# A decoder layer on one core: unread banks at set boundaries, a planner that counts two more kinds of work, a bias load on another queue, and half a scaling on another engine

## The chip, the cores and the metric

The kernel runs on 1 core of one Trainium2 chip. The metric is the device time of one execution in microseconds (us). Engines are named as in the profile: PE (TensorE matmul), PEld (its weight loads), DVE (VectorE), ACT (ScalarE), POOL (GpSimd) and SP (SyncE, which here only issues transfers). L12 is line 12 of the kernel before.

## The reference

One layer of a decoder on a sequence of 256 tokens and 2048 channels, in float32: a SwiGLU FFN of width 5632, a mixer with two branches, and a second FFN. A conditioning vector gives nine rows of modulation (`mod`).

```python
mod = (silu(c) @ w_ada + b_ada).reshape(B, 9, 1, D)
h = modulate(rms_norm(x, g_ffn1), mod[:, 0], mod[:, 1])
x = x + 0.5 * mod[:, 2] * swiglu(h, w_ffn1_gu, w_ffn1_down)

h = modulate(rms_norm(x, g_mix), mod[:, 3], mod[:, 4])
u_pool, q, k, v, ga, gb = split(h @ w_in)
y_pool = multiscale_pool(u_pool, pool_mix, pool_scale) @ w_pool_up
y_attn = swa_sink_attention(q, k, v, q_gain, k_gain, sinks, rel_bias) @ w_attn_up
x = x + mod[:, 5] * ((sigmoid(ga) * y_pool + sigmoid(gb) * y_attn) @ w_o)

h = modulate(rms_norm(x, g_ffn2), mod[:, 6], mod[:, 7])
x = x + 0.5 * mod[:, 8] * swiglu(h, w_ffn2_gu, w_ffn2_down)
```

The attention is causal in a window of 128 tokens, in blocks of 128, with 16 heads of 64 channels over 2 key heads, a relative-position bias and one sink logit per head in the softmax.

## The kernel before, in words

**Matmuls in three terms.** Every large product goes through `Set.mm` (L296). A weight tile that has been loaded (`raw`) is cut into a rounded high half `wh` (ACT, L277) and the rest `wl` (DVE, L281); the activations lie as high and low halves too (`hh`, `hl`, or `sh`, `sl` made in L385 and L386). PE computes hi x wh, lo x wh and hi x wl. A *set* is one product of 256 tokens with up to 1024 columns: four banks of the accumulator memory (PSUM) of 512 columns, two for each half of the tokens. The inner dimension goes in *ktiles* of 128 rows; a ktile of a full set is 12 matmuls with 512 columns, one of a 512-column set is 6. There are eight banks in two groups of four. A set has one group, the next set the other; small products in between (sums for the modulation, transposes, attention) take their banks from the group that the current set does not use (`bank`), which is the group that the next set will take.

**The written order.** The scheduler is off: each engine runs its instructions in the order in which the code issues them. `push` queues a ktile's matmuls and runs the *turn* of the ktile two before it (`LAG = 2`): its matmuls, and then whatever was filed under that turn's number with `at(n, f)`. So between the L281 of ktile n + 2 and that of ktile n + 3 DVE runs the extra work of turn n. There are three buffers of `wh` and of `wl`, six of `raw` (`RAW`), three of the scratch tag `t2`.

**Set boundaries.** `ends` holds the turn of each set's last ktile. `hop(n, f, g)` files a product f at turn n and the reading of its bank g at n + 1, and moves both on while n is in `ends`. `with_bank` does the same with a fresh bank.

**The modulation.** mod is a product with one row; DVE does it: for each of 16 slabs of `w_ada` one L223, which adds raw times a scalar to an accumulator `acc` of up to 1024 columns (these are called rows of `w_ada` below; the first of an accumulator may be L221). Then the 128 partitions are summed: `halves` (ACT L186, DVE L187), two matmuls with ones (`prod`, L192 and L193), and `use`: for mod 2, 5 and 8 (the gates) ACT copies the bank into `gate` (L199); for the others `mod_col` turns it into a column of channels with four or five DVE operations (L165, L168, L172 or L174 and L175). For gates POOL clears the accumulator and adds the bias row (L214, L215).

**The planner.** `ada_plan(js, n0)` spreads the rows over turns: `room[n]` (2.6 for a full ktile) less `busy[n]` is what DVE has free, in us, by prices written in the code: 1.22 for a wl, 1.28 for a row, and so on, entered with `will`. `spread` gives out turns as the free time adds up. The price of halves and of the columns is not entered. The first FFN plans mod 2, 4, 3 and the first 1024 columns of 7; the mixer plans mod 5, 6 and the rest of 7; the second FFN plans mod 8. The first FFN ends its gate and up products in narrow sets of 512 columns.

**The mixer** runs these sets: q, k and v (256 columns), u, and then twice: a gate of 1024 columns (GA), pool_up (8 ktiles), a gate (GB), attn_up (8 ktiles); then w_o. `heads(n, g)` files a pair of heads, eight times: the load of the bias (L1095, issued by SP, from a table in DRAM) at turn n - 1, the logits at n and their bias adds (L1057, L1058) at n + 1, the maxima at n + 2, the exponentials (ACT L1072) at n + 3, `over` at n + 4 (reciprocal and four scalings, L1076 to L1080, DVE), the transposes at n + 5 (L1085; copied by ACT, L1092, a turn later), and for each second pair the product with v at n + 7 with its copies (L1122, DVE) at n + 8. There is one bias tile, so the load of a pair waits until DVE has read the bias of the pair before.

**Transitions** from the first FFN to the mixer and from the mixer to the second FFN are written out by hand (`transition`).

Of the kernel before, what the change touches and what calls it, by code (L numbers as in the profile page):

```python
# [16 lines left out]
P = 128  # L17
# [17 lines left out]
T2 = 3  # L35
TAIL = 4
TA, TB = 5, 4
NS = 7
LAG = 2
ROOM = 2.6  # L40


@with_exitstack
def trunk_layer(ctx, tc, x, c, w_ada, b_ada, g_ffn1, w_ffn1_gu, w_ffn1_down, g_mix, w_in,
# [78 lines left out]

    def hop(n, f, g):

        while n in ends:
            n += 1
        at(n, f)
        at(n + 1, g)
# [46 lines left out]

    def ada_plan(js, n0):

        def sums(j, c0, a, n, o):
            got = []

            def halves():
                hi, lo = t_([P, CW], "t2", T2, F32R), t_([P, CW], "t2", T2, F32R)
                nc.scalar.copy(hi, a[0][:, o:o + CW])  # L186
                nc.vector.tensor_tensor(lo, a[0][:, o:o + CW], hi.bitcast(F32), ALU.subtract)  # L187
                got.extend((hi, lo))

            def prod():  # L190
                got.append(bank())
                nc.tensor.matmul(got[2], ones, got[0], start=True, stop=False)  # L192
                nc.tensor.matmul(got[2], ones, got[1], start=False, stop=True)  # L193

            def use():
                if j % 3 == 2:
                    if j not in gates:
                        gates[j] = t_([P, D], "gate", 1)
                    nc.scalar.activation(gates[j][:, c0 + o:c0 + o + CW], got[2], AF.Copy, scale=1.0 if j == 5 else 0.5)  # L199
                else:  # L200
                    mod_col(j, got[2], c0 + o)

            at(n, halves)
            hop(n + 2, prod, use)

        for j, c0, a_w in js:
            a, r, nk = [], [], 2 * SW // a_w
            where = spread(n0, KD, 1.28 * a_w / SW)
            for kk, n in enumerate(where):
# [15 lines left out]
                at(n, go)  # L225
                will(n, 1.28 * a_w / SW)
            n0 = n
# [314 lines left out]
    def ffn(w_gu, w_down, hh, hl, actT, f0, sg, g, jgate, after, js):  # L542
# [13 lines left out]
        for f in range(f0, DFF, SW):  # L556
            u = min(SW, DFF - f) / SW
            for i in range(KD * (1 if first else 2) - (TB if g is not None and f == f0 else 0)):
                room[n], busy[n] = ROOM * u, busy.get(n, 0.0) + 1.22 * u
                n += 1  # L560
# [5 lines left out]
        for i in range(2 * KF):  # L566
            will(n + i, 1.22 + (0.34 if i < KF or not 4 <= i - KF < 4 + KD else 0.0))
# [286 lines left out]
    def toe_out():  # L854
# [55 lines left out]
    for n in range(nQ, W1 + KD - TA):  # L910
        u = 0.26 if nK <= n < nU else 1.0
        room[n] = ROOM * u
        will(n, 1.22 * u)
        if any(a <= n < a + 8 for a in Y + A) or n >= W0:
            will(n, 0.34)
# [32 lines left out]

    def with_bank(n, shape, f, g):

        b = []
        hop(n, lambda: (b.append(bank(shape)), f(b[0])), lambda: g(b[0]))

# [42 lines left out]
    with_bank(nU + 11, (P, CW), k_turn,  # L996
              lambda b: nc.scalar.activation(kT.rearrange("p a b -> p (a b)"), b, AF.Copy, scale=gq[:, 1:2]))
    with_bank(nU + 12, (P, S), v_turn, lambda b: nc.scalar.copy(vR.rearrange("p a b -> p (a b)"), b))

# [43 lines left out]
    def heads(n, g):  # L1043
# [31 lines left out]
        def over():  # L1075
            nc.vector.tensor_tensor(dn, sm, es, ALU.add)  # L1076
            nc.vector.reciprocal(rc, dn)
            for i in range(2):
                for blk, (a, e) in enumerate(spans):
                    nc.vector.tensor_scalar_mul(l[:, i, a:e], l[:, i, a:e], rc[:, blk, i:i + 1])  # L1080

# [6 lines left out]
        def turned(i):  # L1088
            def f(b):
                if g % 2 == i == 0:  # L1090
# [3 lines left out]

        at(n - 1, lambda: nc.sync.dma_start(bias, bass.AP(tensor=toe[:].tensor, offset=toe[:].offset + h0 * TOE,  # L1095
                                                          ap=[[1, P], [TOE, 2], [1, S]])))
# [23 lines left out]
        for blk in range(2):  # L1120
            with_bank(n + 7, (P, 2, P), out_prod(blk),
                      lambda b, blk=blk: nc.vector.tensor_copy(attnT[:, g - 1:g + 1, blk * P:(blk + 1) * P], b))  # L1122
        will(n + 8, 0.8)

# [165 lines left out]
```

## Time and profile before

| what | value |
|---|---|
| median of 3 runs | 2011.06 us (2009.54 to 2015.25) |
| the profiled execution's own time | 2012.3 us |
| its span, first to last instruction | 2010.5 us |
| mean granted clock of PE | 0.998 |
| busy: PE, DVE, ACT, POOL | 1977.7, 1515.2, 1084.2, 20.1 us |
| read from memory (HBM) | 520.00 MB, 260 GB/s over the span |
| first FFN, about | 27 to 775 us |
| mixer, about | 775 to 1277 us |
| second FFN, about | 1277 us to the end |

The profile gives the busy time of each engine, the idle time ahead of each group of instructions with what ended it (`<-`), and who waited for whom. A busy PE is not PE at its peak: the end of a matmul is modelled, and matmuls overlap. Idle time of an engine that the others do not wait for costs nothing. The time of a single execution contains 1.8 us around the span.

### The profile page before, as it was taken

What the parts mean: (1) busy time and instruction counts of PE and PEld (TensorE: products, weight loads), DVE (VectorE), ACT (ScalarE), POOL (GpSimd) and SP (SyncE); (2) the same over time, 40 slices, a digit from 0 to 9 for tenths busy, and PEclk for the clock granted to TensorE, in tenths of its full rate; (3) what the DMA queues carried; (4) which work ended last, traced back from release to release, by engine and by line L of the source; (5) the groups of instructions that cost most, each with busy time, mean ns of one, the idle gap of its engine ahead of it and who ended that gap; (6) DMA issues with size and microseconds to landing.
All of it is one profiled execution on the core that took longest, in us unless ns stands there. A gap on an engine that the chain in (4) does not pass through costs nothing.

```text
span 2010.5 us, 23739 instructions
## 1 busy us (share of the span) xinstructions
PE 1977.7 (98%) x8873; PEld 1629.0 (81%) x8873; DVE 1515.2 (75%) x1759; ACT 1084.2 (54%) x1469; POOL 20.1 (1%) x42
## 2 busy tenths in 40 slices
PE   7999999999999999999999999999999999999998
PEld 5788888888788878887778888888788888888887
DVE  6888877989999988876799996888455454565655
ACT  5544457664655446445556455645554645565443
POOL 1000000000000000000000000000000000000000
PEclk9999999999999999999999999999999999999999
DMA  9989745899899976764698984688555545476652
GB/s 355 381 304 336 261 165 188 329 348 367 320 364 346 326 257 236 292 228 153 232 339 304 370 321 158 225 335 327 212 198 189 210 176 198 152 228 214 218 185 74
DMA packets 159603, 523.67 MB, mean 260 GB/s; under 512 B 9309, under 2 KB 23285, under 8 KB 159232
## 3 DMA queue, kind: packets, MB, share of 16 engines
q1 hardware_dynamic: 158496, 520.92, 72.3%
q8 instruction: 69, 1.13, 0.2%
q0 software_dynamic: 992, 1.24, 0.2%
q14 instruction: 46, 0.38, 0.1%
HBM read 520.00 MB, written 2.12 MB: 260 GB/s over the span
## 4 chain that ended last, share of the span: by engine, by line
PE 89%; DVE 5%; DMA 3%; ACT 1%; issue 1%; SPq 0%; ACTq 0%; DVEq 0%
PE bank L296 86%; DVE wl L281 2%; DMA raw<-in_w_in_dram 1%; DVE acc L223 1%; DMA raw<-in_w_pool_up_dram 1%; ACT wh L277 1%; DMA raw<-in_w_ada_dram 1%; DVE acc L649 0%; PE bank L1024 0%; SPq L641 0%; PE bank L792 0%; DMA raw<-in_w_ffn_down_dram 0%; PE bank L349 0%; PE bank L192 0%; DVE mcol L168 0%
## 5 line engine op out<-in xcount | busy, mean ns | idle before, releaser
L277 ACT CAST wh<-raw 128x1024 fp32r<-128x1024 f32 (+2 forms) x712 | 710.6, 1001 | 805.0 <-PE bank L296 709.8
L281 DVE TENSOR_TENSOR wl<-raw,wh 128x1024 fp32r<-128x1024 f32 (+2 forms) x713 | 822.3, 1156 | 416.5 <-ACT wh L277 409.9
L296 PE MATMUL bank<-wh,hl 128*128 128x512 f32 (+1 forms) x2088 | 654.8, 389 | 0.0
L296 PE MATMUL bank<-wh,hh 128*128 128x512 f32 (+1 forms) x2064 | 651.6, 391 | 2.5 <-ACT gate L199 1.4
L296 PE MATMUL bank<-wl,hh 128*128 128x512 f32 (+1 forms) x2064 | 647.8, 389 | 2.4 <-DVE wl L281 2.3
L296 PEld LDWEIGHTS bank<-wh,hl 128*128 128x128 f32 x2088 | 392.6, 188 | 81.9 <-DVE hl L833 0.5
L296 PEld LDWEIGHTS bank<-wl,hh 128*128 128x128 f32 x2064 | 387.9, 188 | 85.2 <-DVE wl L281 5.1
L296 PEld LDWEIGHTS bank<-wh,hh 128*128 128x128 f32 x2064 | 385.8, 188 | 82.2 <-ACT gate L199 1.9
L223 DVE SCALAR_TENSOR_TENSOR acc<-raw,cs,acc 128x1024 f32<-128x1024 f32 (+1 forms) x231 | 279.4, 1209 | 3.6 <-DMA raw<-in_w_ada_dram 2.8
L296 PE MATMUL bank<-wh,sh 128*128 128x512 f32 x656 | 204.8, 392 | 2.8 <-DVE big L1122 2.7
L296 PE MATMUL bank<-wh,sl 128*128 128x512 f32 x656 | 204.3, 391 | 1.0 <-DVE sl L386 0.9
L296 PE MATMUL bank<-wl,sh 128*128 128x512 f32 x656 | 203.9, 390 | 0.8 <-DVE wl L281 0.8
L296 PEld LDWEIGHTS bank<-wh,sh 128*128 128x128 f32 x656 | 122.8, 188 | 29.4 <-ACT wh L277 3.1
L296 PEld LDWEIGHTS bank<-wh,sl 128*128 128x128 f32 x656 | 122.9, 188 | 28.8 <-DVE sl L386 3.4
L296 PEld LDWEIGHTS bank<-wl,sh 128*128 128x128 f32 x656 | 123.3, 188 | 27.2 <-DVE wl L281 1.3
L534 ACT COPY big<-raw 32x512 f32<-32x512 f32 (+1 forms) x208 | 121.8, 586 | 4.3
L649 DVE SCALAR_TENSOR_TENSOR acc<-raw,cs,acc 128x1024 f32<-128x1024 f32 (+2 forms) x74 | 77.6, 1050 | 3.1 <-DMA raw<-in_w_ada_dram 2.1
L386 DVE TENSOR_TENSOR sl<-big,sh 128x512 fp32r<-128x512 f32 x82 | 56.1, 684 | 0.0
L385 ACT CAST sh<-big 128x512 fp32r<-128x512 f32 x82 | 50.6, 617 | 0.0
L756 DVE TENSOR_TENSOR big<-bank,big 128x512 f32<-128x512 f32 x56 | 36.4, 682 | 0.0
L187 DVE TENSOR_TENSOR t<-acc,t 128x512 fp32r<-128x512 f32 x28 | 19.2, 687 | 11.2 <-PE bank L192 9.4
L186 ACT CAST t<-acc 128x512 fp32r<-128x512 f32 x28 | 17.3, 617 | 10.3 <-DVE acc L223 10.1
(213 smaller groups left out, 792.1 us busy)
## 6 DMA issues: line engine op xcount, KB each, us to landing
raw<-in_w_ffn_gu_dram SPq DMA_DIRECT2D x175, 1024.0 KB, 5.4
raw<-in_w_ada_dram SPq DMA_DIRECT2D x112, 1024.0 KB, 7.7
raw<-in_w_ffn_down_dram SPq DMA_DIRECT2D x86, 1024.0 KB, 5.9
raw<-in_w_in_dram SPq DMA_DIRECT2D x48, 1024.0 KB, 7.2
raw<-in_w_ada_dram SPq DMA_DIRECT2D x64, 512.0 KB, 7.9
raw<-in_w_o_dram SPq DMA_DIRECT2D x15, 1024.0 KB, 6.2
raw<-in_w_pool_up_dram SPq DMA_DIRECT2D x8, 1024.0 KB, 8.9
raw<-in_w_attn_up_dram SPq DMA_DIRECT2D x8, 1024.0 KB, 8.1
```

The source lines that it names most:

```text
L186: nc.scalar.copy(hi, a[0][:, o:o + CW])
L187: nc.vector.tensor_tensor(lo, a[0][:, o:o + CW], hi.bitcast(F32), ALU.subtract)
L223: nc.vector.scalar_tensor_tensor(out=a[0], in0=r[0][:, kk % nk, :], scalar=sc, in1=a[0], op0=ALU.mult, op1=ALU.add)
L277: nc.scalar.copy(wh, raw_k)
L281: nc.vector.tensor_tensor(wl[:, e], raw_k[:, e], wh[:, e].bitcast(F32), ALU.subtract)
L296: nc.tensor.matmul(self.banks[t][i], a[:, sl], w[:, o], start=first and q == 0, stop=last and q == 2)
L385: nc.scalar.copy(hi, src[:, k:k + n, :])
L386: nc.vector.tensor_tensor(lo, src[:, k:k + n, :], hi.bitcast(F32), ALU.subtract)
L534: nc.scalar.copy(actT[32 * j:32 * j + 32, k:k + m, :].rearrange("p k (t i r) -> p k t i r", t=T, i=4)[:, :, :, i, :], z[0][32 * i:32 * i + ...
L649: nc.vector.scalar_tensor_tensor(out=acc, in0=r, scalar=sc, in1=acc, op0=ALU.mult, op1=ALU.add)
L756: nc.vector.tensor_tensor(a, b, a, ALU.add)
```

## The change

1. `hop` gets `early`: then it also moves on while the reading turn n + 1 is a set's last ktile. The sums of the modulation and the attention's product with v use it. The transposes of q, and the products that turn k and v, are filed one turn later.
2. The planner enters 0.65 for halves and 1.7 for columns, prices a row at 1.24 and a wl at 1.18, and in the FFNs gives at most 1.3 us of a full ktile to rows (`ROWS`). Columns 512 to 1023 of mod 7 move from the first FFN's plan to the mixer's.
3. The bias is loaded by POOL.
4. Of the four scalings of a pair's probabilities two go to ACT, and all four to turn n + 5; transposes and the product with v are filed one turn later.

```diff
+ROWS = 1.3
...
-    def hop(n, f, g):
-        while n in ends:
+    def hop(n, f, g, early=False):
+        while n in ends or early and n + 1 in ends:
             n += 1
         at(n, f)
         at(n + 1, g)
...
-    def spread(n, m, cost):
+    def spread(n, m, cost, cap=9.0):
         out, left = [], 0.0
         while len(out) < m:
-            left = min(left, 2 * cost) + max(0.0, room.get(n, ROOM) - busy.get(n, 0.0))
+            r = room.get(n, ROOM)
+            left = min(left, 2 * cost) + max(0.0, min(r - busy.get(n, 0.0), r * cap / ROOM))
...
             at(n, halves)
-            hop(n + 2, prod, use)
+            hop(n + 2, prod, use, True)
+            will(n, 0.65)
+            if j % 3 != 2:
+                will(n + 3, 1.7)
...
-            where = spread(n0, KD, 1.28 * a_w / SW)
+            where = spread(n0, KD, 1.24 * a_w / SW, cap)
...
-        ada_plan(js, pushed[0])
+        ada_plan(js, pushed[0], ROWS)
...
-            [(j, c, SW) for j in (2, 4, 3) for c in (0, SW)] + [(7, 0, CW), (7, CW, CW)])
+            [(j, c, SW) for j in (2, 4, 3) for c in (0, SW)] + [(7, 0, CW)])
...
-        pair_T(nU + 9 + a // 4, lambda t, f: q_sb[:, t, f * P:(f + 1) * P], a, q_dst)
+        pair_T(nU + 10 + a // 4, lambda t, f: q_sb[:, t, f * P:(f + 1) * P], a, q_dst)
...
         def over():
             nc.vector.tensor_tensor(dn, sm, es, ALU.add)
             nc.vector.reciprocal(rc, dn)
-            for i in range(2):
-                for blk, (a, e) in enumerate(spans):
-                    nc.vector.tensor_scalar_mul(l[:, i, a:e], l[:, i, a:e], rc[:, blk, i:i + 1])
+
+        def parts():
+            for blk, (a, e) in enumerate(spans):
+                nc.scalar.mul(l[:, 0, a:e], l[:, 0, a:e], rc[:, blk, 0:1])
+                nc.vector.tensor_scalar_mul(l[:, 1, a:e], l[:, 1, a:e], rc[:, blk, 1:2])
...
-        at(n - 1, lambda: nc.sync.dma_start(bias, bass.AP(tensor=toe[:].tensor, offset=toe[:].offset + h0 * TOE,
+        at(n - 1, lambda: nc.gpsimd.dma_start(bias, bass.AP(tensor=toe[:].tensor, offset=toe[:].offset + h0 * TOE,
...
-        do(n + 4, 1.2, over)
+        do(n + 4, 0.3, over)
+        do(n + 5, 0.5, parts)
         for i in range(2):
-            with_bank(n + 5, (P, TOE), turn(i), turned(i))
+            with_bank(n + 6, (P, TOE), turn(i), turned(i))
...
-            with_bank(n + 7, (P, 2, P), out_prod(blk),
-                      lambda b, blk=blk: nc.vector.tensor_copy(attnT[:, g - 1:g + 1, blk * P:(blk + 1) * P], b))
-        will(n + 8, 0.8)
+            with_bank(n + 8, (P, 2, P), out_prod(blk),
+                      lambda b, blk=blk: nc.vector.tensor_copy(attnT[:, g - 1:g + 1, blk * P:(blk + 1) * P], b), True)
+        will(n + 9, 0.8)
...
-    ada_plan([(j, c, SW) for j in (5, 6) for c in (0, SW)] + [(7, SW, SW)], nQ)
+    ada_plan([(j, c, SW) for j in (5, 6) for c in (0, SW)] + [(7, CW, CW), (7, SW, SW)], nQ)
```

The lines of the changed kernel are shifted: up to `spread` by a few, from L281 (there L286) on by five, in `heads` by five to eight.

The first place is DVE in the narrow set that ends the first FFN's up product (512 columns; `wl` is a weight half, `t`, `bank` and `mcol` belong to the columns of mod 4, `acc` to a row). Before:

```order
L281 TENSOR_TENSOR wl_3926<-raw_3876,wh_3925 128x512
L165 TENSOR_TENSOR t_706_3935<-bank_3921,ident 128x512
L168 TENSOR_REDUCE mcol<-t_706_3935 128x4
L174 SCALAR_TENSOR_TENSOR mcol<-mcol,bcol 128x4
L175 TENSOR_TENSOR mcol<-mcol,gcol 128x4
L281 TENSOR_TENSOR wl_3947<-raw_3944,wh_3946 128x512
L165 TENSOR_TENSOR t_711_3956<-bank_3940,ident 128x512
L168 TENSOR_REDUCE mcol<-t_711_3956 128x4
L174 SCALAR_TENSOR_TENSOR mcol<-mcol,bcol 128x4
L175 TENSOR_TENSOR mcol<-mcol,gcol 128x4
L223 SCALAR_TENSOR_TENSOR acc_3888<-raw_3961,cs,acc_3888 128x1024
```

And the same columns in the changed kernel, three ktiles further on:

```order
L286 TENSOR_TENSOR wl_3955<-raw_3924,wh_3954 128x512
L167 TENSOR_TENSOR t_711_3964<-bank_3946,ident 128x512
L170 TENSOR_REDUCE mcol<-t_711_3964 128x4
L176 SCALAR_TENSOR_TENSOR mcol<-mcol,bcol 128x4
L177 TENSOR_TENSOR mcol<-mcol,gcol 128x4
L286 TENSOR_TENSOR wl_3970<-raw_3924,wh_3969 128x512
L226 TENSOR_SCALAR acc_3982<-raw_3983,cs 128x1024
L286 TENSOR_TENSOR wl_3990<-raw_3987,wh_3989 128x512
L167 TENSOR_TENSOR t_720_3999<-bank_3979,ident 128x512
L170 TENSOR_REDUCE mcol<-t_720_3999 128x4
L176 SCALAR_TENSOR_TENSOR mcol<-mcol,bcol 128x4
L177 TENSOR_TENSOR mcol<-mcol,gcol 128x4
```

Two sets of columns behind neighbouring weight halves, the second with a row, have become two sets with a ktile between them that holds the first row of the next accumulator.

The second place is DVE at the boundary from the first GA set to pool_up (`sl` belongs to pool_up's first ktile, `am` to the softmax, `big` holds logits and the attention's output, L1057 and L1058 are the bias adds of the fourth pair). Before:

```order
L281 TENSOR_TENSOR wl_7454<-raw_7451,wh_7453 128x1024
L386 TENSOR_TENSOR sl_7458<-big_6186,sh_7457 128x512
L1076 TENSOR_TENSOR am<-am 128x4
L1077 RECIPROCAL am<-am 128x4
L1080 TENSOR_SCALAR big_6186<-big_6186,am 128x256
L1080 TENSOR_SCALAR big_6186<-big_6186,am 128x128
L1080 TENSOR_SCALAR big_6186<-big_6186,am 128x256
L1080 TENSOR_SCALAR big_6186<-big_6186,am 128x128
L281 TENSOR_TENSOR wl_7494<-raw_7451,wh_7493 128x1024
L1122 COPY big_6186<-bank_7473 128x2x128
L1122 COPY big_6186<-bank_7476 128x2x128
L1057 TENSOR_TENSOR big_6186<-bank_7487,big_6186 128x256
```

In the changed kernel:

```order
L286 TENSOR_TENSOR wl_7419<-raw_7416,wh_7418 128x1024
L391 TENSOR_TENSOR sl_7423<-big_6149,sh_7422 128x512
L1081 TENSOR_TENSOR am<-am 128x4
L1082 RECIPROCAL am<-am 128x4
L228 SCALAR_TENSOR_TENSOR acc_6939<-raw_7448,cs,acc_6939 128x1024
L286 TENSOR_TENSOR wl_7452<-raw_7416,wh_7451 128x1024
L1087 TENSOR_SCALAR big_6149<-big_6149,am 128x256
L1087 TENSOR_SCALAR big_6149<-big_6149,am 128x128
L1062 TENSOR_TENSOR big_6149<-bank_7442,big_6149 128x256
L1063 TENSOR_TENSOR big_6149<-bank_7442,big_6149 128x128
L1062 TENSOR_TENSOR big_6149<-bank_7445,big_6149 128x256
L1063 TENSOR_TENSOR big_6149<-bank_7445,big_6149 128x128
```

The copies of the attention output have left the boundary (they stand two weight halves further on), a row of `w_ada` stands where the four scalings stood, two scalings stand a weight half later, and the bias adds are where they were.

The third place is SP in the same stretch, where `big<-toe` is the bias and the others are weights. Before:

```order
L1095 DMA big_6186<-toe 128x2x256
L253 DMA raw_7335<-in_w_in_dram 128x2x1024
L218 DMA raw_7364<-in_w_ada_dram 128x2x1024
L253 DMA raw_7393<-in_w_in_dram 128x2x1024
L1095 DMA big_6186<-toe 128x2x256
L253 DMA raw_7451<-in_w_pool_up_dram 128x2x1024
L253 DMA raw_7517<-in_w_pool_up_dram 128x2x1024
```

In the changed kernel:

```order
L258 DMA raw_7299<-in_w_in_dram 128x2x1024
L223 DMA raw_7331<-in_w_ada_dram 128x2x1024
L258 DMA raw_7356<-in_w_in_dram 128x2x1024
L258 DMA raw_7416<-in_w_pool_up_dram 128x2x1024
L223 DMA raw_7448<-in_w_ada_dram 128x2x1024
L258 DMA raw_7477<-in_w_pool_up_dram 128x2x1024
```

The bias loads no longer stand between the weight loads; all eight stand on POOL between two pairs of L214 and L215.

More of the change, by code (lines that the diff above doesn't have):

```diff
@@ L558, in ffn @@
             for i in range(KD * (1 if first else 2) - (TB if g is not None and f == f0 else 0)):
-                room[n], busy[n] = ROOM * u, busy.get(n, 0.0) + 1.22 * u
+                room[n], busy[n] = ROOM * u, busy.get(n, 0.0) + 1.18 * u
                 n += 1
@@ L566, in ffn @@
         for i in range(2 * KF):
-            will(n + i, 1.22 + (0.34 if i < KF or not 4 <= i - KF < 4 + KD else 0.0))
+            will(n + i, 1.18 + (0.34 if i < KF or not 4 <= i - KF < 4 + KD else 0.0))
         for i in range(4):
             will(n + KF - 1 + 2 * i, 1.36)
-        ada_plan(js, pushed[0])
+        ada_plan(js, pushed[0], ROWS)
         while f0 < DFF:
@@ L947, in qk_scale, with with_bank @@
         nc.vector.tensor_tensor(k3, k3, qs[:, 5, t, NH:NQK].unsqueeze(2).to_broadcast([P, NKV, HD]), ALU.mult)
-    def with_bank(n, shape, f, g):
+    def with_bank(n, shape, f, g, early=False):
         b = []
-        hop(n, lambda: (b.append(bank(shape)), f(b[0])), lambda: g(b[0]))
+        hop(n, lambda: (b.append(bank(shape)), f(b[0])), lambda: g(b[0]), early)
     def pair_T(n, src, f0, dst):
```

11 lines of the change are left out of this document (5 added, 6 removed).

## The prediction

> **What bounds the kernel now.** I read the page first, then the waits of TensorE (PE) alone, then the stretches around its longer waits, instruction by instruction.
>
> ```profile
> span 2010.5 us, 23739 instructions
> PE 1977.7 (98%) x8873; PEld 1629.0 (81%) x8873; DVE 1515.2 (75%) x1759; ACT 1084.2 (54%) x1469; POOL 20.1 (1%) x42
> L296 PE MATMUL bank<-wh,hh 128*128 128x512 f32 (+1 forms) x2064 | 651.6, 391 | 2.5 <-ACT gate L199 1.4
> ```
>
> From the stretches (length; busy us of PE, its weight loads, DVE, ACT and POOL, each with its count of instructions; then clock, DMA share, GB/s):
>
> ```profile
> 477.00:532.00 55.00, 52.41 (x228) 42.25 (x227) 52.03 (x70) 33.37 (x53) 0.00 (x0) 1.00 0.88 326
> 900.00:950.00 50.00, 47.29 (x234) 37.81 (x233) 32.00 (x72) 28.53 (x59) 0.00 (x0) 1.00 0.41 143
> 951.00:954.50 3.50, 3.50 (x11) 2.71 (x10) 2.97 (x10) 1.04 (x1) 0.00 (x0) 0.51 0.67 161
> 1420.00:2005.00 585.00, 584.96 (x2581) 484.02 (x2579) 314.80 (x308) 300.68 (x363) 2.19 (x4) 1.00 0.55 187
> ```
>
> PE sets the time. From 1420 us on it has no hole, and 585/2581 = 0.227 us is what a matmul costs in a run; so a full ktile (12 of them) is 2.72 us and one of the narrow set (6) 1.36. What can be gained is what PE waits for before that, and the waits of PE list it (us in total, times, longest):
>
> ```profile
> PE bank L701 <- ACT junk L321: 8.1, 1, 8.1
> PE bank L296 <- DVE wl L281: 3.2, 3, 1.8
> PE bank L296 <- DVE big L1122: 2.7, 1, 2.7
> PE bank L296 <- ACT gate L199: 1.4, 1, 1.4
> PE bank L296 <- DVE sl L386: 0.9, 2, 0.6
> PE bank L1085 <- DVE big L1080: 0.5, 1, 0.5
> PE bank L1085 <- DVE big L1122: 0.3, 1, 0.3
> ```
>
> The first row is the start of the program, which no edit touches. The other six, 9.0 us, are in the stretch that the change plans anew.
>
> **The new plan numbers (halves and modulation columns counted, rows capped, half a column block moved).** This is how the two longest waits on wl came about:
>
> ```profile
> 510.32 0.69 DVE L281 TENSOR_TENSOR wl<-raw,wh 128x512 fp32r<-128x512 f32 x1
> 510.93 0.69 DVE L165 TENSOR_TENSOR t<-bank,ident 128x512 f32<-128x512 f32 x1
> 511.65 0.69 DVE L168 TENSOR_REDUCE mcol<-t 128x4 f32<-128x512 f32 x1
> 512.38 0.17 DVE L174 SCALAR_TENSOR_TENSOR mcol<-mcol,bcol 128x4 f32<-128x4 f32 x1
> 512.58 0.16 DVE L175 TENSOR_TENSOR mcol<-mcol,gcol 128x4 f32<-128x4 f32 x1
> 512.66 1.28 DVE L223 SCALAR_TENSOR_TENSOR acc<-raw,cs,acc 128x1024 f32<-128x1024 f32 x1
> 513.85 1.29 DVE L281 TENSOR_TENSOR wl<-raw,wh 128x512 fp32r<-128x512 f32 x2
> 514.59 0.50 PE L296 MATMUL bank<-wl,hh 128*128 128x512 f32 x1 [1.85 <-DVE wl L281]
> ```
>
> Five operations of the modulation stand between two weight halves of which PE wants one every 1.36 us; none but L223 is in the planner's count. DVE needs 0.69 + 0.69 + 0.69 + 0.17 + 0.16 + 1.28 = 3.7 us there, directly behind an earlier such pair, and is already late: 52.03 us busy of 55.
>
> I price each row of DVE's order with its line's mean in the trace and number the ktiles by their L281 rows. In the narrow set (ktiles 161 to 192) DVE's running sum of work minus 1.36 a ktile stands at 6.3 us before, at the ktile shown; after, the two column sets stand two ktiles apart with one modulation row between, and the sum never passes 4.1. Before passes 4.3 earlier in the same set without a wait, so 4.1 should pass too. In ktiles 248 to 262 (about 677 to 721 us) DVE has 49.1 us before and 41.0 after, against 15 x 2.72 = 40.8 on PE. In 376 to 391 (about 1073 to 1119 us) it is 46.6 and 42.8, against 43.5. So the five waits on wl and sl go: 3.2 + 0.9 = **4.1 us**.
>
> What is pushed back lands in ktiles 424 to 439, ahead of the second transition: 30.5 us of DVE work before, 45.5 after (eight rows of L223, two halves, two column sets more), against 43.5 on PE and two pairs of sums. What hides it is DVE's idle time there:
>
> ```profile
> DVE wl L281 <- ACT wh L277: 17.3, 19, 1.5
> ```
>
> That is from 1210 to 1290 us, 17.3 against the 15.0 added; DVE is also up to two ktiles (5.4 us) ahead. I cost it at nothing. Were the cover gone, the excess over PE alone, 45.5 - 43.5 = 2.0 us, would show. The smaller plan prices (1.22 to 1.18, 1.28 to 1.24) move rows by one ktile and are in these sums.
>
> **No bank read in the last ktile.** The gate of the last FFN:
>
> ```profile
> 1415.97 0.60 ACT L199 ACTIVATE gate<-bank 128x512 f32<-128x512 f32 x1
> 1416.63 0.73 PE L296 MATMUL bank<-wh,hh 128*128 128x512 f32 x2 [1.44 <-ACT gate L199]
> ```
>
> ACT reads the bank behind four SiLUs of the set that just ended, and the next set's first matmul wants that bank. With the sums moved so that the read falls in the next set, nothing wants it: **1.4 us**. The other is in the mixer (SP issues loads; a row's bracket is its engine's idle time before it):
>
> ```profile
> 936.22 0.37 SPq L1095 DMA_DIRECT2D big<-toe  x1
> 936.67 0.93 SPq L253 DMA_DIRECT2D raw<-in_w_pool_up_dram  x2
> 943.32 1.05 ACT L277 CAST wh<-raw 128x1024 fp32r<-128x1024 f32 x1 [2.30 <-DMA raw<-in_w_pool_up_dram]
> 944.40 1.23 DVE L281 TENSOR_TENSOR wl<-raw,wh 128x1024 fp32r<-128x1024 f32 x1 [2.97 <-ACT wh L277]
> 948.61 0.75 DVE L1122 COPY big<-bank 128x256 f32<-128x256 f32 x2
> 949.50 0.94 PE L296 MATMUL bank<-wh,sh 128*128 128x512 f32 x2 [2.71 <-DVE big L1122]
> ```
>
> PE waits 2.71 us for copies of the attention output, which now come two ktiles later. But the bias adds of the fourth head pair still stand in that set's last ktile and hold two of the four banks, so this wait goes only if DVE is earlier, and that is the bias edit's part. **2.7 us**, less 0.5 that I leave for those adds (a pair is 0.42 + 0.28 = 0.70 us, rows below).
>
> The granted clock was 0.51 in the 3.5 us after that wait, a loss of 3.5 x 0.49 = **1.7 us**. I let it go with its wait. The Trainium skill (TensorE: Matmul & The Clock Gate, Part 1) has the array fall to half its clock after an idle window of about 3.4 us; by that a wait of 2.71 is too short and the sum would be 1.7 less. The trace shows the half clock right behind the wait and decides.
>
> **Bias on GpSimd's queue.** SP is held at L1095 until DVE has read the old bias, and the weight loads stand behind it (the L277 row is of 850 to 1040 us):
>
> ```profile
> SPq L1095 <- DVE big L1058: 72.2, 7, 13.5
> ...
> L277 ACT CAST wh<-raw 128x1024 fp32r<-128x1024 f32 x54 | 56.4, 1048 | 70.5 <-PE bank L296 46.8 <-DMA raw<-in_w_in_dram 16.6 <-DMA raw<-in_w_pool_up_dram 4.1
> L1057 DVE TENSOR_TENSOR big<-bank,big 128x256 f32<-128x256 f32 x16 | 6.7, 416 | 0.7 <-PE bank L1052 0.7
> L1080 DVE TENSOR_SCALAR big<-big,am 128x256 f32<-128x256 f32 x16 | 5.6, 351 | 0.3
> L1058 DVE TENSOR_TENSOR big<-bank,big 128x128 f32<-128x128 f32 x16 | 4.5, 280 | 0.0
> ```
>
> 72.2 us in seven waits, while the transfer engines were 0.41 busy (900 to 950). The pool_up load went out at 936.67 and ACT had it at 943.32, 2.30 us late, which became DVE's 2.97 and PE's 2.71. With the bias off SP, the loads go when a buffer is free, up to 13.5 us earlier. GpSimd now waits for the old bias instead; behind it stand only the accumulators of the last FFN's gate (L214, L215), a stage away. Eight issues of 0.37 us leave SP: nothing, SP is not the bound.
>
> **Half the scaling on ACT, transposes one ktile later.** DVE loses half of L1080: 8 x (0.351 + 0.280 (taken from L1058, of one size)) = 5.0 us. ACT gains 16 operations. ACT's own scaled ones over the same data (L1072) bound each from above:
>
> ```profile
> L1072 ACT ACTIVATE big<-big,am 128x256 f32<-128x256 f32 x16 | 7.9, 494 | 0.0
> L1072 ACT ACTIVATE big<-big,am 128x128 f32<-128x128 f32 x16 | 6.2, 387 | 0.0
> ```
>
> 8 x (0.494 + 0.387) = 7.0 us at most; below, DVE's own price, 5.0. I take 7.0. ACT is idle 46.8 us there merely because its buffers are full, which hides it. ACT now waits for DVE's reciprocal, with the next wh queued behind; the reciprocal is emitted a ktile earlier, so that wait is short, and the wh has two ktiles to spare. The transposes' waits, 0.5 + 0.3 = **0.8 us**, I halve: 0.4.
>
> **The sum.** 4.1 + 1.4 + 2.7 + 1.7 + 0.8 = 10.7. Each ended wait also saves the restart: a lone matmul shows 0.39 us where one in a run takes 0.227, 0.16 for each of nine waits, 1.5. Less 0.5 (adds) and 0.4 (transposes): 11.3, say **11 us**. The profiled execution took 2012.3 us (span 2010.5 and 1.8 around it), 1.2 above the median of 2011.06; it would take 2001.3, and the median comes to **2000 us**.
>
> **The rivals.** *The boundary wait stays (0.13).* The change does not do all it says there: two banks are still read in the last ktile, and DVE's way to them has a row of L223 (1.28) in place of scaling. Against it: DVE's own lateness came from the load. It would keep 2.7 + 1.7 + 0.2 and the transposes' 0.4: gain 6, 2005.
>
> *The backlog only moves (0.08).* The rows are as many as before, and the transfers are already 0.88 busy around the wait at 514 (477 to 532, above). If loads or the fuller ktiles 424 to 439 bring the waits on wl back, 4.1 + 5 x 0.16 is lost: gain 6.1, 2005. Against it: PE has no wait in that stretch, and the first FFN now has 4 MB less to load.
>
> *Slower: the bias comes late (0.03).* On GpSimd's queue a transfer of the bias's size took longer than on SP's:
>
> ```profile
> big<-toe SPq DMA_DIRECT2D x8, 256.0 KB, 4.5
> ...
> out_dram<-x_sb POOLq DMA_DIRECT2D x4, 256.0 KB, 5.2
> ```
>
> (KB each, us to landing.) DVE's next add would wait, and the weight halves behind it. Two ktiles of lead (5.4 us) and three between head pairs (8.2) cover 13.6; from there each us shows eight times. A tie needs 11/8 = 1.4 more, a landing of 15.0 us; at 16.5 it is 2.9 x 8 - 11 = 12 us slower, 2023. Nothing in the trace lands so late. The Trainium skill (SBUF — State Buffer, SBUF: two separate sides) speaks against this edit: while VectorE runs an operation that takes both ports, GpSimd cannot write the descriptors, and a transfer of 620 ns became 3100. As an estimate from that page each bias would be 2.5 us later, which those 13.6 us still cover; no run here shows it.
>
> **How the numbers follow.** The forecast has 0.76. Its own range is 1997 (all 12.2 and 2 of small pauses) to 2003. The two partial cases, 2005, move the upper end to 2008; below, 1996.5 takes in a median half a us lower. About 0.04 lies above and some below. What a measurement of this kernel can tell from no change is about 0.3%, 6 us. Faster by more: the forecast, and half of the 0.21 of the partial cases, which stand at 6: 0.86. Within: the other half, 0.10. Slower: 0.03, and 0.01 for what I don't see.
>
> **What would show it.** Right: in the waits of PE, no row of L199 or of the output copies, wl and sl under 1 us together; no stretch of half clock near 950; SP's waits without L1095, and ACT's 16.6 on w_in mostly gone; DVE's idle time from 1210 to 1290 down from 17.3 to a few us with no wait of PE there. Wrong: a PE wait on the bias adds at the same boundary, new waits on wl ahead of the second transition, or DVE waiting for big<-toe.

## The result, and the profile after

The changed kernel took 2001.38 us (median of 5, 1999.77 to 2001.68), the kernel before, in the same series, 2015.25 (median of 5, 2009.54 to 2016.45): a ratio of 0.9937 (95% interval 0.9920 to 0.9953). The forecast was 2000. Of the five runs of the kernel before two lie at 2009.5 and 2011.1 and three at 2015.3 to 2016.5, so the medians lie 13.9 us apart; the two profiled spans lie 10.6 apart, near the 11 us that were forecast. The waits are not quite as foreseen. The page of the changed kernel begins:

```profile
span 1999.9 us, 23744 instructions
PE 1973.2 (99%) x8873; PEld 1628.4 (81%) x8873; DVE 1512.1 (76%) x1743; ACT 1089.9 (54%) x1485; POOL 26.0 (1%) x50
```

The span is 10.6 us shorter. The waits of PE (us in total, times, longest), of which the rows of the program's start are left out but for one:

```profile
PE bank L706 <- ACT junk L326: 8.0, 1, 8.0
...
PE bank L301 <- DVE wl L286: 2.1, 4, 0.9
...
PE bank L1122 <- DVE big L1176: 1.2, 1, 1.2
...
PE bank L195 <- DVE t L189: 0.3, 1, 0.3
```

The gate (L199), the copies of the attention output, the transposes and the waits on sl are gone from the list. L1122 (the product with v) and L195 (a sum of the modulation) are new. Of the four waits on wl (at 64, 518, 822 and 884 us) only the one at 518 stands where the kernel before had one. The stretches of before, at the same times of the clock:

```profile
900.00:950.00 50.00, 50.00 (x246) 40.27 (x244) 36.06 (x75) 34.38 (x72) 2.90 (x4) 1.00 0.66 225
951.00:954.50 3.50, 3.50 (x18) 2.85 (x16) 2.10 (x5) 2.62 (x6) 0.00 (x0) 1.00 1.01 396
477.00:532.00 55.00, 54.42 (x238) 43.95 (x237) 50.30 (x69) 34.70 (x55) 0.00 (x0) 1.00 0.83 305
```

From 900 to 950 us PE is full (47.29 before), the transfer engines are 0.66 busy (0.41 before), and there is no half clock behind it. In the narrow set PE is busy 54.42 of 55 us (52.41 before). ACT's wait for weights in the mixer, POOL's wait in place of SP's, the landing time of the bias, and DVE's idle time ahead of the second transition, each from its own view:

```profile
L282 ACT CAST wh<-raw 128x1024 fp32r<-128x1024 f32 x56 | 58.6, 1049 | 68.0 <-PE bank L301 54.3 <-issue 8.5 <-DMA raw<-in_w_in_dram 5.2
```

```profile
POOL big L1102 <- DVE big L1063: 104.1, 7, 26.3
```

```profile
big<-toe POOLq DMA_DIRECT2D x8, 256.0 KB, 4.7
```

```profile
DVE wl L286 <- ACT wh L282: 3.2, 6, 1.2
```

POOL waits 104.1 us where SP waited 72.2, and past the start of the program no other engine waits for POOL; DVE never waits for `big<-toe`. ACT's 16.6 us on w_in are 5.2, DVE's 17.3 idle us are 3.2, as foreseen.

**Time by stage.** Executions of even the same code differ by some us at their start (last section). So I compare three stages of each trace: from the product with the position table (L852, here L857, near 373 us) to the first transpose of the first transition (L349, here L354); from there to the first transpose of the second transition (the mixer); and from there to PE's last matmul. With 16 rows fewer in the first FFN and 16 more in the mixer, one sum's products move with them, some 0.45 us.

| kernel | first FFN | mixer | second FFN | sum |
|---|---|---|---|---|
| before | 401.2 | 503.1 | 727.2 | 1631.5 |
| changed | 396.2 | 499.5 | 725.5 | 1621.1 |
| before + bias on POOL | 401.2 | 496.0 | 727.2 | 1624.4 |
| before + moved reads (part 1) | 402.3 | 505.7 | 726.1 | 1634.1 |
| before + new plan (part 2) | 396.5 | 511.0 | 725.5 | 1633.0 |
| before + plan + bias | 396.4 | 499.5 | 725.5 | 1621.4 |
| changed, bias on SP | 396.2 | 507.9 | 725.6 | 1629.6 |
| changed, bias on ACT | 396.4 | 499.4 | 725.5 | 1621.3 |
| changed, scaling undone (part 4) | 396.7 | 503.7 | 725.5 | 1625.9 |
| changed, product with v later | 396.1 | 500.6 | 725.6 | 1622.3 |
| changed, halves moved | 396.2 | 497.7 | 725.6 | 1619.4 |
| changed, product later, halves moved | 396.1 | 498.8 | 725.6 | 1620.5 |
| changed, halves moved, early drain | 396.2 | 497.6 | 725.6 | 1619.4 |
| changed, halves moved, scaling undone | 396.6 | 503.0 | 725.5 | 1625.1 |

In the stages that an edit does not reach, these times agree within 0.6 us in the first FFN (396.1 to 396.7 with the new plan) and within 0.1 in the second.

### The profile page after: what moved, and what is told of

Read it like the earlier page. It is cut to its first block, busy times and chain, and to the rows that moved or that the text cites. A ratio compares the mean times of both kernels' runs of the same rounds, so it can differ in the third digit from the quotient of the medians.

```text
span 1999.9 us, 23744 instructions
## 1 busy us (share of the span) xinstructions
PE 1973.2 (99%) x8873; PEld 1628.4 (81%) x8873; DVE 1512.1 (76%) x1743; ACT 1089.9 (54%) x1485; POOL 26.0 (1%) x50
## 4 chain that ended last, share of the span: by engine, by line
PE 94%; DVE 3%; DMA 1%; ACT 1%; issue 1%; SPq 0%; DVEq 0%; ACTq 0%
PE bank L301 91%; DVE wl L286 1%; DMA raw<-in_w_ada_dram 1%; DVE acc L654 1%; DMA raw<-in_w_ffn_gu_dram 1%; PE bank L1029 0%; SPq L646 0%; PE bank L797 0%; PE bank L194 0%; ACT wh L282 0%; PE bank L195 0%; PE bank L354 0%; PE bank L1092 0%; PE bank L1056 0%; PE bank L1015 0%
## 5 line engine op out<-in xcount | busy, mean ns | idle before, releaser
L286 DVE TENSOR_TENSOR wl<-raw,wh 128x1024 fp32r<-128x1024 f32 (+2 forms) x713 | 822.9, 1156 | 405.2 <-ACT wh L282 398.3
L391 DVE TENSOR_TENSOR sl<-big,sh 128x512 fp32r<-128x512 f32 x82 | 56.1, 684 | 0.0
L326 ACT ACTIVATE junk<-x_sb 128x512 bf16<-128x512 f32 x24 | 15.2, 632 | 15.2 <-DVE x_sb L418 13.1
```

What stands on the lines that cost most here:

```text
L286: nc.vector.tensor_tensor(wl[:, e], raw_k[:, e], wh[:, e].bitcast(F32), ALU.subtract)
L326: nc.scalar.activation(junk, x_sb[:, t, n * CW:(n + 1) * CW], AF.Square, scale=(D / 2) ** -0.5, accum_out=ssq[:, t, n:n + 1])
L391: nc.vector.tensor_tensor(lo, src[:, k:k + n, :], hi.bitcast(F32), ALU.subtract)
```

## The two new waits, in the trace

The first is at the end of mod 5's accumulator. DVE's view, and then PE's row:

```profile
872.92 1.22 DVE L286 TENSOR_TENSOR wl<-raw,wh 128x1024 fp32r<-128x1024 f32 x1 [1.19 <-ACT wh L282]
881.12 0.69 DVE L189 TENSOR_TENSOR t<-acc,t 128x512 fp32r<-128x512 f32 x1 [6.97 <-PE bank L194]
881.73 1.28 DVE L228 SCALAR_TENSOR_TENSOR acc<-raw,cs,acc 128x1024 f32<-128x1024 f32 x1
882.93 1.22 DVE L286 TENSOR_TENSOR wl<-raw,wh 128x1024 fp32r<-128x1024 f32 x1
```

```profile
884.20 0.74 PE L301 MATMUL bank<-wl,hh 128*128 128x512 f32 x2 [0.91 <-DVE wl L286]
```

DVE stands 6.97 us at the second half of a sum, with two ktiles of lead gone: it needs a buffer of `t2`, there are three, each sum holds two until its product has run (L194), and `early` has moved that product past a boundary but not the halves of the next sum. The weight half behind it is late, and PE waits 0.91 (and 0.32 for the sum itself).

The second is in the first turn after pool_up, DVE and PE in order of time:

```profile
968.57 1.28 DVE L1176 TENSOR_TENSOR big<-bank,big 128x512 f32<-128x512 f32 x2
...
971.54 1.22 DVE L286 TENSOR_TENSOR wl<-raw,wh 128x1024 fp32r<-128x1024 f32 x1
...
972.12 0.65 PE L1125 MATMUL bank<-sg,big 128*64 128x256 f32 x4
...
972.67 1.28 DVE L1176 TENSOR_TENSOR big<-bank,big 128x512 f32<-128x512 f32 x2
...
974.01 0.66 PE L1122 MATMUL bank<-sg,big 128*64 128x256 f32 x4 [1.24 <-DVE big L1176]
```

DVE reads pool_up's four banks (L1176) in two pairs, a turn apart. The second product with v (head pairs three and four) was filed at turn 21 and is now at 24: part 4 files it one turn later, at 22, and `early` moves it past 23, the last turn of pool_up. There it takes its banks from the group that pool_up has just left, and the second one has not been read.

## The experiments

**The bias alone.** In the kernel before:

```diff
-        at(n - 1, lambda: nc.sync.dma_start(bias, ...
+        at(n - 1, lambda: nc.gpsimd.dma_start(bias, ...
```

> The kernel before with one edit: the bias is loaded by POOL. My theory (load): PE's 2.71 us wait at the boundary from GA to pool_up comes from weight loads held on SP behind the bias. Then the wait shrinks to 0.5 us or less although the copies of the attention output stay in the last ktile, the half clock behind it goes, SP's waits lose the 72.2 us, and the gain is 2.7 + 1.7 + 0.2 - 0.5 = 4.1 us, about 2007. Rival (banks): the wait comes from where the copies stand; then 1.5 us or more of it stay and the gain is at most 1.5 us, 2009.5 or more. Rival (late bias): DVE waits for the bias in the records, and the time is 2011 or more. All else, the gate's 1.4 and the waits on wl and sl, stays.

2004.89 us, ratio 0.9961 (0.9948 to 0.9973). PE's waits past the start:

```profile
PE bank L296 <- DVE wl L281: 3.1, 3, 1.9
...
PE bank L296 <- ACT gate L199: 1.4, 1, 1.4
PE bank L296 <- DVE sl L386: 0.9, 2, 0.5
```

The boundary wait is gone though the copies of the attention output and the bias adds both still stand in the last ktile, and so are both waits of the transposes, though all four scalings are on DVE a turn earlier. The mixer is 7.1 us shorter, not 4.1. SP had stood longer at the bias than the 72.2 us that I counted: in the kernel before it also waited there for the landing of the bias before.

```profile
SPq L1095 <- DMA big<-toe: 18.2, 6, 3.7
```

The rival (banks) falls: where the banks are read did not matter at that boundary once the loads were in time.

**Part 1 alone.** In the kernel before, `hop` with `early` for the sums and the product with v, and the turns of q, k and v:

```diff
-        while n in ends:
+        while n in ends or early and n + 1 in ends:
...
-            hop(n + 2, prod, use)
+            hop(n + 2, prod, use, True)
```

> The kernel before with part 1 alone: no bank of the sums and of the product with v is read in a set's last ktile; q, k and v are turned one ktile later. Both theories: the gate's wait at 1415 goes, 1.4 + 0.16 us. Theory (load): DVE is still late at the boundary, and the bias adds of the fourth pair stand in the last ktile, so PE waits there for L1057 or L1058 1.5 us or more; about 2009. Theory (banks): that wait is under 0.5 us and the half clock goes, 2.7 + 1.7 more; about 2005. In either case DVE's waits at the second half of a sum (L187 for L192) grow from 9.4 to about 17 us, as in the changed kernel, since the products are moved and the halves are not.

2015.54 us, ratio 1.0012 (1.0003 to 1.0021). Its wait at the boundary, and DVE's at a sum's second half:

```profile
PE bank L296 <- DVE big L1058: 4.4, 1, 4.4
```

```profile
DVE t L187 <- PE bank L192: 20.6, 7, 6.5
```

The wait does not go; it grows from 2.7 to 4.4 us, on the bias adds, which were next. The gate's wait goes, but the halves, 20.6 us instead of 9.4, bring waits of 0.9 on wl and 0.3 on a sum near 1040 us.

**Part 2 alone.** Prices, counts, cap and the moved half block, as in the diff above.

> The kernel before with part 2 alone: the planner's new prices, counts, cap and the moved half block. My theory: the five waits on wl and sl (3.2 + 0.9 us) fall to 1 us or less, with their restarts 3.9 to 4.9 us gained, about 2006.5; the boundary wait and the gate's 1.4 stay. Rival (the backlog only moves): PE waits on wl come back somewhere else, ahead of the second transition or in the mixer, 3 us or more in all, and the time is 2009 or more.

2014.04 us, ratio 1.0002 (0.9993 to 1.0011):

```profile
PE bank L301 <- DVE big L1063: 5.6, 1, 5.6
...
PE bank L301 <- DVE hl L391: 2.0, 2, 1.0
```

Each was right in part: the waits on wl and sl fall to 1.2 us as my theory has it, and the time is the rival's. The first FFN gains 4.7 us, the second 1.7: the plan moves the sums of mod 8 too, and with them the gate's wait, which I had expected to stay. But the mixer, which gets the 16 rows, is 7.9 us longer: 5.6 at the boundary instead of 2.7, half clock for 6.8 us behind it instead of 3.4, 1.6 us more at the transposes, and two waits of 1.0 on the activations of the second transition.

**The bias back on SP.** In the changed kernel the first edit reversed.

> The changed kernel with one part undone: the bias is loaded by SP again. Theory (load): SP is held for about 70 us again, loads of the mixer come late, and PE waits 1.5 us or more at the boundary from GA to pool_up or on wl in the mixer; 2.5 to 4.6 us slower than the changed kernel, 2004 to 2006. Theory (banks): the copies have left the last ktile, so nothing waits; within 1 us of the changed kernel's 2001.4.

2011.23 us, ratio to the kernel before 0.9991 (0.9982 to 1.0000). PE's waits, then SP's:

```profile
PE bank L301 <- DVE big L1063: 4.1, 2, 3.7
...
PE bank L1122 <- DVE big L1176: 2.8, 1, 2.8
```

```profile
SPq L1102 <- DVE big L1063: 74.0, 7, 13.5
```

The mixer loses 8.4 us, more than the theory gave. Parts 1, 2 and 4 without part 3 are worth hardly anything that these runs can tell.

**The bias on ACT's queue.** In the changed kernel `nc.scalar.dma_start` for `nc.gpsimd.dma_start`.

> The changed kernel with the bias loaded by ACT instead of POOL. Theory (queue): what cost was that SP stands and cannot issue the weights; any engine that issues no weights will do. ACT then waits for DVE's read of the old bias with its next wh behind, which is at most a few us in seven waits; within 1 us of the changed kernel. Rival (who waits matters): ACT's wait holds wh, DVE's wl and PE behind it: 2 us or more slower than the changed kernel, with waits of PE on wh or wl in the mixer.

2002.08 us, ratio 0.9945 (0.9932 to 0.9957); every stage within 0.3 us of the changed kernel. The bias landed in 3.4 us:

```profile
big<-toe ACTq DMA_DIRECT2D x8, 256.0 KB, 3.4
```

So it is not POOL's queue that brings the gain, but that SP, which issues the weights, no longer stands. Landing in 3.4 or in 4.7 us made no difference.

**The halves moved too.** In the changed kernel the halves of a sum's second columns are not filed before the product of its first:

```diff
-            hop(n + 2, prod, use, True)
+            p = hop(n + 2, prod, use, True)
...
+            return p
...
-                sums(j, c0, a, n + 1 + 2 * i, i * CW)
+                p = sums(j, c0, a, max(p, n + 1 + 2 * i), i * CW)
```

> The changed kernel, and the halves of a sum's second 512 columns are not filed before the product of its first: early moves the products of mod 5 past a boundary, the halves stay, and DVE stands 6.97 us at L189 because all three buffers of t2 are taken. My theory (buffer): with the halves moved too, that wait of DVE goes, and with it PE's 0.32 on L189 and 0.91 on wl; with restarts 1.5 us gained, span 1998.4. Rival (work): DVE's rows there are too many for the ktiles, and the wait on wl stays at 0.5 us or more; span 1999.3 or more.

1998.28 us, ratio 0.9930 (0.9918 to 0.9942). DVE's wait at the halves, and PE's waits on wl (lines of `sums` are one lower):

```profile
DVE t L188 <- PE bank L193: 8.7, 8, 1.8
```

```profile
PE bank L301 <- DVE wl L286: 1.2, 3, 0.6
```

The 6.97 us are gone, with the 0.91 and the 0.32 behind them: the mixer falls by 1.8 us, as the buffer theory said.

**The product with v a turn later.** In the changed kernel:

```diff
-            with_bank(n + 8, (P, 2, P), out_prod(blk),
+            with_bank(n + (11 if g == 3 else 8), (P, 2, P), out_prod(blk),
```

> The changed kernel, and the second pair's product with v (fourth head pair) one ktile later, at turn n + 11 instead of n + 8, which early had made n + 10. My theory (early bank): the new 1.24 us wait of L1122 on L1176 in the changed kernel is there because early moves the product into the first turn after pool_up, where DVE has not yet read that set's banks; with the product one ktile later the wait goes, 1.24 + 0.16 us gained, span 1998.5. Rival (DVE late): DVE is behind there anyway, and the wait comes back on another bank, on wl or on the transposes; span within 0.5 of 1999.9. The waits near 882 us stay.

2002.42 us, ratio 0.9946 (0.9934 to 0.9959). My theory fell. The wait came back, on the transposes of the fifth pair, which stand in the same turn and now took that bank:

```profile
PE bank L1092 <- DVE big L1176: 1.5, 1, 1.5
```

With 0.6 more on ACT behind it the mixer is 1.1 us longer. Both edits together:

> Both edits, of the product and of the halves, on the changed kernel. If the two waits are separate, the gains add: span 1997.0, 2.9 us under the changed kernel. If one takes the place of the other, 1998.4 or more.

2001.29 us, ratio 0.9942 (0.9928 to 0.9956); the mixer -0.7 for -1.8 and +1.1: they add, but one is a loss.

**All four banks of pool_up read at once**, on top of the moved halves:

```diff
-            at(B[half_] - 1 + q // 2, lambda t=t, i=i, f=pooled: f(t, i), True)
+            at(B[half_] - 1, lambda t=t, i=i, f=pooled: f(t, i), True)
```

> The changed kernel with the halves moved (as in the run that did so alone: mixer 497.7 us), and all four banks of pool_up read at the set's last turn instead of two there and two a turn later. If the new wait is only that a bank of the second two is wanted before DVE reads it, it goes and the mixer is 496.3 us, near the 496.0 that the kernel before has with the bias edit alone. Rival (DVE late): the reads that now stand ahead of the maxima and a weight half push the wait on, to wl or to the transposes, 0.7 us or more; mixer 497 or more. The rest of the program as in the changed kernel: the first FFN after 373 us 396.2, the second 725.5.

2000.64 us, ratio 0.9942 (0.9929 to 0.9954). The wait moved a second time, to the logits of the next pair, which want the bank of the product with v:

```profile
PE bank L1056 <- DVE big L1130: 1.0, 1, 1.0
```

The mixer, 497.6, is as without it. In each of the three orders that were run PE waits for something there: in the changed kernel DVE has, between 965 and 978 us, the bias adds, the maxima and the four reads beside its weight halves. Whether fewer of them in these ktiles would end it was not tried.

**Plan and bias together**, without parts 1 and 4:

> The kernel before with the bias on POOL and the new plan, without the moved reads and without the scaling on ACT. With the plan alone the mixer took 511.0 us, 7.9 more than before; with the bias alone 496.0. Theory (the rows that the plan moves into the mixer cost only because SP is held): mixer 496 to 497. Rival (the rows cost by themselves): mixer 499 or more, with waits at the boundary near 942 on the bias adds or on hl ahead of the second transition. The first FFN after 373 us 396.2 in both; the gate's wait of the second FFN is gone by the plan already, since the products move with their rows: 725.5.

2001.97 us, ratio 0.9950 (0.9936 to 0.9963). PE's and DVE's waits that matter:

```profile
PE bank L301 <- DVE hl L391: 2.0, 2, 1.0
```

```profile
DVE t L167 <- PE bank L195: 2.0, 1, 2.0
```

The boundary is free, but the mixer is 3.4 us longer than with the bias alone. The rival is right: the rows cost by themselves, 2.0 us of it ahead of the second transition. The sum, 1621.4, is the changed kernel's 1621.1.

**Part 4 undone.** In the changed kernel all four scalings in `over` on DVE at n + 4, transposes at n + 5, product at n + 7.

> The changed kernel with part 4 undone: all four scalings on DVE at n + 4, transposes at n + 5, the product with v at n + 7. Theory (part 4 makes the new wait): the second pair's product then stands at turn 21 and is read at 22, so early does not move it past pool_up's end, the transposes of the fifth pair stand at 22 as well, and nothing wants a bank of pool_up in turn 24. The 1.24 us wait goes; the mixer, from the first transition's first transpose to the second's, falls from 499.5 to about 498.0 us; no wait of PE on scaling comes, since the loads are in time. Rival (DVE needs the relief): DVE's 5 us more make waits on wl, on the scalings or at the boundary near 942, 1 us or more in all, and the mixer stays at 499 or more.

2006.64 us, ratio 0.9970 (0.9959 to 0.9981). Both theories hold in part. The 1.24 us wait goes, as mine said; but more is lost at a place that neither named, 2.6 us on L440, 1.0 on the activations (L391) behind it, and 1.7 because the clock is 0.50 for 3.4 us after that:

```profile
PE bank L301 <- DVE wl L440: 2.6, 1, 2.6
```

```profile
1249.41 0.69 DVE L167 TENSOR_TENSOR t<-bank,ident 128x512 f32<-128x512 f32 x1
...
1255.91 0.69 DVE L167 TENSOR_TENSOR t<-bank,ident 128x512 f32<-128x512 f32 x1 [4.70 <-PE bank L195]
...
1257.63 1.23 DVE L440 TENSOR_TENSOR wl<-raw,wh 128x1024 fp32r<-128x1024 f32 x1
```

`over` enters 1.2 us a pair at the planner instead of 0.3 + 0.5, so the rows are given out later: the last one starts 35.7 us ahead of the second transition's first transpose, against 46.0 in the changed kernel. The last columns of mod 7 then fall into the set's end, `early` pushes their product on, DVE waits 4.70 us for it, and the weights of the transition (L440) stand behind it. This kernel is that of the plan and the bias together (above) with part 1 added and nothing else: 503.7 against 499.5 us in the mixer. With the halves moved as well it is the same:

> The changed kernel with the halves moved and part 4 undone. If both new waits are what they seem, mixer 496.3 us, and the whole some 3 us under the changed kernel, as with the earlier reads of pool_up's banks. If DVE needs part 4's relief, 498 or more.

2004.12 us, ratio 0.9961 (0.9948 to 0.9973): the mixer 503.0, and PE again waits 2.6 us on L440, here with half clock for 6.8 us behind it.

## Why the prediction was right, and where it was not

**The plan, 4.1 us and restarts: right.** The first FFN is 5.0 us shorter, some 0.45 of it products that moved to the mixer. One reading was wrong: that the backlog in the narrow set never passes 4.1 us and goes without a wait.

```profile
518.67 0.50 PE L301 MATMUL bank<-wl,hh 128*128 128x512 f32 x1 [0.57 <-DVE wl L286]
```

Priced again over the rows of both traces, each by its group's mean, from the first L281 of 512 columns on and less 1.36 a ktile, the running sum is 8.1 us at the place shown of the kernel before (I had 6.3) and 5.4 ahead of this wait. That is over the 4.3 that had passed.

**"What hides it is DVE's idle time there": held, but by part 4.** The 15.0 us ahead of the second transition cost no wait in the changed kernel. With the scaling back on DVE they cost some 5 us there, well over the 2.0 that I gave as the price if the cover went; without part 1 as well (plan and bias together) they cost 2.0. I had costed part 4 as 0.4 us at the transposes; its real worth, 4.2 us in the mixer, is that DVE's 5 us, and their lower price at the planner, make room for the rows in time. ACT's side was sized well, 7.0 us foreseen and 4.0 + 3.1 measured:

```profile
L1086 ACT ACTIVATE big<-big,am 128x256 f32<-128x256 f32 x8 | 4.0, 504 | 0.0
L1086 ACT ACTIVATE big<-big,am 128x128 f32<-128x128 f32 x8 | 3.1, 389 | 0.0
```

**The gate, 1.4 us: right size, shared cause.** The second FFN is 1.7 us shorter, the wait and its restart. But the plan alone takes it away too, so with both parts it is counted once.

**The bias and the boundary: right cause, too small.** I took 2.7 - 0.5 + 1.7, 0.4 at the transposes and the restarts, some 4.8 in all. The bias alone gives 7.1. Both traces have the same 8873 matmuls in the same order, and counted along them the kernel before falls 2.9 us behind at the wait, 1.9 in the half clock and the first transposes, which stand in it, and the other 2.2 at later transposes (964 to 1014 us). The bias edit gave the transposes' gain, not part 4, and nothing had to be left for the bias adds.

**The step that failed: a moved read, "nothing wants it".** That held for the gate's read. For the others I asked only what they leave, and put what they meet at nothing; a new wait at the boundary I looked for at the bias adds alone. The products that `early` moves land in the first turn after a boundary, where half of the old set's banks are not read yet (1.24 us), and they leave behind halves that fill the buffers of `t2` (1.23 us, 1.8 with what goes with it). My sign "wl and sl under 1 us together" failed, with 2.1 us, and for this only in part: with the halves moved 1.2 are left, at 64, 518 and 822 us. In the mixer the changed kernel lies 3.4 us above the bias alone: 2.5 are these waits, 0.35 the wait at 822 us, which every kernel with the new plan has, and 0.45 the products that moved there.

**Part 1 paid nothing.** I had the gate's 1.4 us and a share of the boundary from it. The plan alone takes away the one and the bias alone the other. Plan and bias without parts 1 and 4 are as short as the whole change (1621.4 and 1621.1 in the table). On top of them part 1 costs 4.2 us, 1.7 of it half clock, and part 4 gives these back. The change with part 1 alone left out was not run.

So the mechanisms of the plan and the bias were right, but that the sum came out was luck: two errors cancel, the bias 2.3 us more than I said, and 3.4 in the mixer that I had at nothing. In the table: -5.0 (plan, first FFN), -1.7 (gate), -7.1 (bias), +3.4 (the rest of the change in the mixer), -10.4 in all. The rivals: the boundary wait did stay in each kernel that had the bias on SP, and larger; with the whole change it did not. The backlog came back ahead of the second transition in each kernel with the new plan and without part 4, and in no other. No run shows a late bias.

**The half clock.** In the prediction I let it go with its wait, and it went: with the bias alone the clock of that stretch is 1.00 too.

## What to carry to other kernels

An engine that issues the prefetches should not also issue a load that waits for a consumer: here one such wait took away the lead of all that stood behind it, and the stall showed up much later, on another engine's name. Before a read is moved off a boundary, list what else holds the same banks and buffers at the place where it lands, and move both halves of a pair. Undo each part of a bundle by itself: here one part cost what another gave back, and no total shows that. Relief of a busy engine can be worth more through what a planner then puts earlier than where it is taken. The best version here, by its stages 1.7 us under the changed kernel, is the one with the halves moved (the early drain adds nothing to it), and the whole-run ratios (0.9930 and 0.9937) do not tell these two apart.

## What the runs showed of the hardware

The length of a wait did not decide whether the clock fell. From 66 to 80 us (columns as above; the clock is the third number from the end), the changed kernel, the one with the later product and the one with the moved halves, which are the same code so far, gave:

```profile
66.00:80.00 14.00, 12.49 (x56) 10.42 (x56) 10.00 (x13) 8.22 (x11) 0.00 (x0) 0.88 1.01 383
```

```profile
66.00:80.00 14.00, 12.79 (x65) 10.54 (x64) 10.25 (x14) 8.28 (x11) 0.00 (x0) 1.00 1.03 384
```

```profile
66.00:80.00 14.00, 12.49 (x49) 10.12 (x48) 8.50 (x12) 7.32 (x10) 0.00 (x0) 0.76 1.00 381
```

A wait near 66 us, 1.5, 1.2 and 1.5 us long, was followed by 14 x 0.12 = 1.7, none and 14 x 0.24 = 3.4 us of lost clock. Behind that wait PE has only 16 products with one column for some 1.9 us (L797) before wide ones come again. In the changed kernel with the bias on SP a wait of 2.8 us at 979 was followed by none:

```profile
979.00:993.00 14.00, 11.22 (x61) 8.41 (x61) 10.73 (x24) 6.55 (x16) 0.00 (x0) 1.00 0.28 89
```

The Trainium skill (TensorE: Matmul & The Clock Gate, Part 1) calls the window in which the array's activity is watched free-running, not started by the kernel. These rows fit that, since the same wait has different ends. The starts of the low stretches fit it too: within each trace they lie a whole number of 3.413 us apart (70.43 and 951.07 us in the kernel before, 258 of them). On that grid, the stretch ahead of the half clock of the kernel before and the clock behind it, and then the same for the 2.8 us wait with the bias on SP:

```profile
947.66:951.07 3.41, 1.56 (x6) 1.14 (x7) 3.41 (x8) 3.02 (x6) 0.00 (x0) 1.00 0.01 2
951.07:954.48 3.41, 3.41 (x11) 2.62 (x10) 2.88 (x10) 1.04 (x1) 0.00 (x0) 0.50 0.67 162
```

```profile
977.97:981.38 3.41, 1.66 (x9) 0.76 (x7) 3.27 (x10) 1.40 (x7) 0.00 (x0) 1.00 0.98 284
981.38:984.79 3.41, 2.38 (x17) 1.79 (x18) 2.85 (x6) 2.27 (x7) 0.00 (x0) 1.00 0.18 74
```

What separates the cases is how much of a wait falls into one stretch of the grid, not its length, and the stretch need not be idle as a whole. Past 40 us in all 14 traces, each stretch at full clock in which PE was busy with products wider than one column for 1.3 us or less was followed by half clock, and none with 1.66 us or more was; the two between went one each way (1.47 us kept the clock, 1.56 lost it). So whether the boundary wait cost 1.7 us more hung on where the grid cut it, which is chance, and spans of single runs differ by up to 3.4 us for this alone, which is why the table starts at 373 us.

The Trainium skill's warning of late transfers on GpSimd's queue (SBUF — State Buffer, SBUF: two separate sides) did not bear here: 4.7 us to landing on POOL's queue, 4.5 on SP's in the kernel before, and 4.4 in the kernel before with the bias on POOL.
